# Values of two heads projected as a pair, token blocks stationary, in a one-core decoder layer

## The chip, the core and the metric

The kernel runs on one core of one Trainium2 chip. The metric is device time in microseconds, lower is better. Before the change it took 2126.11 us, the median of three runs that lie between 2125.86 and 2126.69 us.

## The reference, cut to what matters

One layer on 512 tokens of width 2048, all in float32: RMS norm, one wide input projection, 16 attention heads of 128 columns, output projection with residual, RMS norm, gated feed-forward network with residual.

```python
proj = h @ w_in          # h = rms_norm(x); columns are split by head
qf, kf, vf, ff, qn, kc, vc, ks, vs, kw, vw, gt = jnp.split(proj, cuts, axis=-1)
# 8 "fox" heads: q, k normalised per head, forgetting attention
qf = _rms_norm(qf.reshape(B, T, Hf, Dh), fox_q_norm)
kf = _rms_norm(kf.reshape(B, T, Hf, Dh), fox_k_norm)
vf = vf.reshape(B, T, Hf, Dh)                       # values: no norm
# 8 "nsa" heads in 2 groups: compressed (kc, vc), selected (ks, vs) and
# window (kw, vw) branches, summed with sigmoid gates gt
o_nsa = g[..., 0:1] * o_c + g[..., 1:2] * o_s + g[..., 2:3] * o_w
x = x + concat(o_fox, o_nsa) @ w_out
x = x + (silu(h2 @ w_gate) * (h2 @ w_up)) @ w_down  # h2 = rms_norm(x)
```

There are twelve value projections: `vs` and `vw` for each of the two groups, and `vf` for each of the eight fox heads.

## The kernel before, in words

Every matrix is split into a high part (rounded to the matmul's reduced float32 form) and a low part (the rest), and a product is three matmuls: high by high, high by low, low by high (`mm3`, L146 to L150). The split takes one ScalarE copy and one VectorE subtraction (`split`, L128; the lines of the profile are L80 and L77, in the helpers `act` and `tt`).

The input is held transposed, in 16 chunks `xg[k]` of 128 columns by 512 tokens, inside one large tile `bigm`. A projection of one head (`proj` and `gemm_steps`) streams its weights in two loads of 128x1024 (`load_w`: three landing buffers `ws`, two split buffers `wp`). Each 128x128 weight block is the stationary operand and the 512 tokens move: 16 chunks by 3 products are 48 matmuls of 512 columns. The result stands in PSUM as head columns by tokens, in one of two banks `g`. `scaled` (L270) multiplies it on VectorE by the tokens' row factor `rstd`. Queries and keys then pass `normed`: square, sum over columns by a matmul with ones (`ss`, L232 and L233), `rsqrt` (three ScalarE steps L222 to L224, three VectorE steps L225 to L227), gain (L295), split. Values need tokens on the partitions, so `value` transposes the scaled tile with four TensorE transposes (`vT`, L310) into a PSUM bank `t` and splits that.

The attention part runs in a written order of generators. `weave` interleaves the steps of a projection with those of an attention head, `stagger` starts the next projection before the rest of the last one (`POST`) is done, `run` takes all steps at once. A scheduling layer places the instructions of each engine, and on each engine they execute in that order. The order before: `ks0`; `vs0`, `kw0`, `vw0` beside the compression of `kc` and `vc` (`windows`, `compress`, whose matmuls `z` are L410); `qn0` beside the gates; the nsa heads 0 to 3, each beside the next projection; `vs1`, `kw1`, `vw1`, `qn4` one after the other; nsa heads 4 to 7; then for each fox head its query, key and value projection beside the attention of the head before. At the end the 16 head outputs are split into `bigm` (these splits wait for the last head's scaled scores, `scores_done`), and the output projection `po` starts, its first two accumulators in the banks `g`.

The feed-forward part behind it (`q`, L976, and `pd`, L1111 and L1116) is not edited. Its matmuls have 256 moving columns, one stationary block each.

Of the kernel before, what the change touches and what calls it, by code (L numbers as in the profile page):

```python
# [17 lines left out]
P = 128  # L18
# [38 lines left out]

SHIFT = 8


# [8 lines left out]
def hybrid_layer(ctx: ExitStack, tc: tile.TileContext, xT, vec, ffb, wfg, wfirst, win, cmpw, wout, wgu, wdn, out):  # L69
# [68 lines left out]

    def load_w(src, name):
# [40 lines left out]
    def gemm_steps(o, srcs, mov, name):  # L180

        k = 0
        for j, src in enumerate(srcs):
            wp = load_w(src, f"{name}_{j}")
            for kk in range(src.shape[-1] // P):
                s = slice(kk * P, (kk + 1) * P)
                mm3(o, wp[:, 0, s], wp[:, 1, s], mov[k][:, 0, :], mov[k][:, 1, :],
                    k == 0, k == len(mov) - 1)
                k += 1
                yield  # L190
        assert k == len(mov)

    def gemm2(os, srcs, mov, name):

        for j in range(4):
            st = wpl.tile([P, HALF * P], F32, tag="ws", name=f"ws_{name}_{j}", bufs=3)
            for i in range(2):
                load(st[:, i * T:(i + 1) * T], srcs[i][j // 2][:, j % 2 * T:(j % 2 + 1) * T])
            wp = wpl.tile([P, 2, HALF * P], FR, tag="wp", name=f"wp_{name}_{j}", bufs=2)
            split(wp, st)  # L200
            for kk in range(4):
                k = 4 * j + kk
                for i in range(2):
                    c = slice(i * T + kk * P, i * T + (kk + 1) * P)
                    mm3(os[i], wp[:, 0, c], wp[:, 1, c], mov[k][:, 0, :], mov[k][:, 1, :], k == 0, k == len(mov) - 1)

# [12 lines left out]

    def rsqrt(dst, src, n, tmp):  # L220
# [5 lines left out]
        nc.vector.tensor_scalar(tmp, tmp, -0.5 / n, 1.5, op0=OP.mult, op1=OP.add)  # L226
        nc.vector.tensor_tensor(dst, dst, tmp, op=OP.mult)  # L227

# [32 lines left out]
    gneg = ap_.tile([P, 2], F32, name="gneg")  # L261
    nc.vector.tensor_scalar_mul(gneg[:, 0:1], v1(V_FQ), -SCALE)
    nc.vector.tensor_scalar_mul(gneg[:, 1:2], v1(V_NQ), -SCALE)

# [18 lines left out]
    def normed(name, gain, tag, bufs):  # L283
# [9 lines left out]
        y = ftile(f"y_{name}")  # L293
        rsqrt(y, o, float(HD), ftile(f"tmp_{name}"))
        nc.vector.scalar_tensor_tensor(t, t, gain, y, op0=OP.mult, op1=OP.mult)  # L295
# [7 lines left out]

    def value(name):

        t = yield from proj(name)
        yield POST
        o = ps.tile([P, T], F32, tag="t", name=f"vT_{name}", bufs=2)
        for i in range(NB):
            nc.tensor.transpose(o[:, i * P:(i + 1) * P], t[:, i * P:(i + 1) * P], ident)  # L310
        r = ap_.tile([P, 2, T], FR, tag="kv", name=name, bufs=5)
        split(r, o)
        live[name] = r

    class Branch:
# [41 lines left out]
        def pv(self, o, start, stop):  # L357
            v, pt = self.v, self.pt
            for n, j in enumerate((0, 1, 3, 2)):
                c = slice(TOFF[j], TOFF[j] + T - j * P)  # L360
                vs = slice(j * P, (j + 1) * P)
                mm3(o[:, j * P:], v[:, 0, vs], v[:, 1, vs], pt[:, 0, c], pt[:, 1, c],
                    start and n == 0, stop and n == NB - 1)
                yield
# [198 lines left out]
    def nsa_q(h):  # L563
        return normed(f"qn{h}", gneg[:, 1:2], "q", 2)

# [8 lines left out]
    for k in range(NK):  # L574
# [5 lines left out]
        split(t, xs, v1(V_AN + k))  # L580
        wp = wpl.tile([P, 2, HALF * P], FR, tag="wp", name=f"w0p_{k}", bufs=2)
        w_done = split(wp[:, :, :T], ws)
        if k == 0:
            wst = wpl.tile([P, HALF * P], F32, tag="ws", name="ws_fg", bufs=3)[:, :NK * 32]
            nc.sync.dma_start(wst, wfg)
            wst = wst.rearrange("p (k c) -> p k c", c=32)
            wf = wpl.tile([P, NK, 2, 32], FR, tag="wp", name="wf", bufs=2)
            nc.scalar.activation(wf[:, :, 0], wst, AF.Copy)
# [15 lines left out]

    ks0 = normed("ks0", v1(V_SK), "kv", 5)
    next(ks0)
    row_rstd("r1")

    def unload():
        for j, which in enumerate(("kc", "vc")):  # L610
# [6 lines left out]
        tokens["fg"] = fg  # L617
        yield

    N, NS, F, FS = 18, 26, 53, 12  # L620
    weave(ks0, unload(), N, 5, 9)
# [3 lines left out]
    weave(nsa_q(0), gates(), N, 4, 2)  # L625
    for h in range(3):
        weave(nsa_q(h + 1), nsa(h), N, NS, 7, 17)
    weave(normed("ks1", v1(V_SK), "kv", 5), nsa(3), N, NS, 7, 17)
# [6 lines left out]
    def qk(h):  # L635
        return stagger(normed(f"qf{h}", gneg[:, 0:1], "q", 2), normed(f"kf{h}", v1(V_FK), "kv", 5))

    weave(qk(0), nsa(7), 2 * N - 1, NS, 6)
    run(stagger(value("vf0")))
    run(late[0])  # L640
    for h in range(NH - 3):
        weave(chain(qk(h + 1), stagger(value(f"vf{h + 1}"))), fox(h), F - 2, FS, 4, 0)

    h = NH - 1
    weave(qk(h - 1), fox(h - 2), 2 * N - 1, FS, 4, 0)
    side = fox(h - 1)
    weave(qk(h), itertools.islice(side, 5), 2 * N - 1, 5, 12)
    weave(stagger(value(f"vf{h - 1}")), itertools.islice(side, 2), N - 1, 2, 8)
    last = fox(h)
    for i, _ in enumerate(stagger(value(f"vf{h}"))):  # L650
        if i in (2, 4, 6, 8, 10):
            next(last)
        if i in (7, 9, 11, 13, 15):
            next(side, None)
    run(late[0])
    run(side)
# [20 lines left out]
    formy = ffp.tile([P, 2 * FORM], FR, tag="fy", name="formy", bufs=1)  # L677

    def cut(m, at, n):
        return m[:, at:at + n]  # L680

# [208 lines left out]
    def load_a(i):  # L890
# [5 lines left out]
        if i == 2:  # L896
            tc.add_manual_dep(d.ins, live["w0"].ins.name, PACE)

    def split2(dst, src):
        h = act(dst[0], src, AF.Copy)  # L900
        tt(dst[1], src, dst[0].bitcast(F32), op=OP.subtract)
        return h

# [308 lines left out]
```

## Time and profile before

| | |
|---|---|
| time of the profiled execution | 2126.17 us |
| its span, first to last instruction | 2124.5 us |
| so outside the span | 1.67 us |
| median of three runs | 2126.11 us |
| TensorE (PE) busy | 2110.1 us, 15135 matmuls |
| VectorE (DVE) busy | 1696.7 us |
| ScalarE (ACT) busy | 996.3 us |
| granted TensorE clock, mean | 0.999 |

Stages by time from the span's start: input and `kc`, `vc`, gate projections to 58 us, the attention part to about 690 us, the output projection to 875 us, gate and up products to 1697 us, down product to the end. In lists of single instructions the first column is the start and the second the duration, both in us. Matmuls are pipelined, so a duration overlaps the next instruction; what a matmul costs is the distance from its start to the next start.

### The profile page before, as it was taken

To read this page: it belongs to the slowest core of one execution; us is meant where nothing else is said; L and a number is where in the kernel's file an instruction comes from. 1 tells how busy PE (TensorE), PEld (TensorE's weight loads), DVE (VectorE), ACT (ScalarE), POOL (GpSimd) and SP (SyncE) were. 2 spreads that over 40 slices of the span, in tenths; PEclk is the share of its full clock that TensorE was granted. 3 is DMA by queue.
4 is the path that set the end of the run, shared out by engine and by line. 5 is a ranking of instruction groups with operands and counts; after the bars stand their busy time and mean duration, and the time that the engine had idled before them with its cause. 6 is when DMAs were issued, how large, how long until landed. Compare 5 with 4: busy or idle time off the path is not lost.

```text
span 2124.5 us, 36976 instructions
## 1 busy us (share of the span) xinstructions
PE 2110.1 (99%) x15135; PEld 1949.7 (92%) x15135; DVE 1696.7 (80%) x2488; ACT 996.3 (47%) x1226; POOL 184.2 (9%) x283
## 2 busy tenths in 40 slices
PE   9999999999999999999999999999999999999998
PEld 7777787888888888999999999999999999999998
DVE  6877568555657454999999999999999987889998
ACT  5555455444446333544344434343443455565553
POOL 0000000111101000111111111111111000000000
PEclk9999999999999999999999999999999999999999
DMA  5421211222222443667676777777777798469864
GB/s 195 149 75 50 61 60 45 85 85 89 86 85 67 157 143 124 169 190 210 185 199 188 186 199 188 200 189 183 204 189 197 230 334 266 150 234 331 291 180 138
DMA packets 113483, 349.57 MB, mean 165 GB/s; under 512 B 13592, under 2 KB 13592, under 8 KB 113312
## 3 DMA queue, kind: packets, MB, share of 16 engines
q1 hardware_dynamic: 85552, 270.33, 38.6%
q0 software_dynamic: 22144, 52.44, 13.5%
q10 hardware_dynamic: 5616, 24.43, 2.9%
q8 instruction: 118, 1.93, 0.4%
q14 instruction: 53, 0.43, 0.1%
HBM read 318.56 MB, written 74.73 MB: 185 GB/s over the span
## 4 chain that ended last, share of the span: by engine, by line
PE 93%; DVE 4%; ACT 2%; issue 1%; DMA 1%; ACTq 0%; SPq 0%; DVEq 0%
PE q L976 39%; PE pd L1111 13%; PE pd L1116 6%; PE po L150 2%; PE po L148 2%; PE po L149 2%; PE ps_kf L148 1%; PE ps_kf L150 1%; PE ps_kf L149 1%; PE ps_qf L148 1%; PE ps_vf L148 1%; PE ps_qf L150 1%; PE ps_qf L149 1%; PE ps_vf L150 1%; PE ps_vf L149 1%; PE ps_qn L150 1%
## 5 line engine op out<-in xcount | busy, mean ns | idle before, releaser
L80 ACT ACTIVATE bigm<-r 128x1792 fp32r<-128x1792 f32 x174 | 298.2, 1714 | 460.4 <-PE q L976 289.9
L77 DVE TENSOR_TENSOR bigm<-r,bigm 128x1792 fp32r<-128x1792 f32 x174 | 351.5, 2020 | 12.1 <-ACT bigm L80 11.5
L77 DVE TENSOR_TENSOR r<-r 128x512 f32<-128x512 f32 x522 | 267.1, 512 | 28.7 <-DMA r<-wgu 16.6
L976 PE MATMUL q<-bigm 128*128 128x256 f32 x1848 | 217.4, 276 | 0.1
L976 PE MATMUL q<-formy,bigm 128*128 128x256 f32 x1848 | 216.8, 276 | 0.0
L976 PE MATMUL q<-forma,bigm 128*128 128x256 f32 x1848 | 216.8, 276 | 0.0
L976 PE MATMUL q<-formx,bigm 128*128 128x256 f32 x1848 | 216.8, 276 | 0.0
L976 PEld LDWEIGHTS q<-bigm 128*128 128x128 f32 x1848 | 213.2, 188 | 0.4 <-DVE bigm L77 0.3
L976 PEld LDWEIGHTS q<-forma,bigm 128*128 128x128 f32 x1848 | 213.0, 188 | 0.1
L976 PEld LDWEIGHTS q<-formy,bigm 128*128 128x128 f32 x1848 | 212.9, 188 | 0.1
L976 PEld LDWEIGHTS q<-formx,bigm 128*128 128x128 f32 x1848 | 212.9, 188 | 0.0
L122 POOL DMA_DIRECT2D wsum<-wdn x176 | 119.8, 687 | 880.5 <-ACT bigm L80 775.9
L1111 PE MATMUL pd<-bigm 128*128 128x256 f32 x1224 | 147.9, 276 | 0.0
L1111 PEld LDWEIGHTS pd<-bigm 128*128 128x128 f32 x1224 | 142.9, 188 | 0.0
L77 DVE TENSOR_TENSOR bigm<-wd,bigm 128x2048 fp32r<-128x2048 f32 (+1 forms) x64 | 110.2, 1723 | 12.9 <-ACT bigm L80 12.7
L80 ACT ACTIVATE bigm<-rawm 128x768 fp32r<-128x768 f32 (+2 forms) x72 | 65.9, 925 | 108.0 <-PE pd L1116 62.7
L148 PE MATMUL po<-bigm,wp_o 128*128 128x512 f32 x256 | 99.9, 390 | 0.7 <-ACT wp_o L80 0.6
L150 PE MATMUL po<-bigm,wp_o 128*128 128x512 f32 x256 | 99.6, 390 | 0.2 <-DVE wp_o L77 0.2
L149 PE MATMUL po<-bigm,wp_o 128*128 128x512 f32 x256 | 99.6, 389 | 0.0
L77 DVE TENSOR_TENSOR bigm<-rawm,bigm 128x768 fp32r<-128x768 f32 (+2 forms) x72 | 75.3, 1055 | 26.4 <-ACT bigm L80 25.6
L80 ACT ACTIVATE bigm<-wd 128x2048 fp32r<-128x2048 f32 (+1 forms) x64 | 93.2, 1456 | 6.0 <-DVE wd L77 2.5
L1116 PE MATMUL pd<-bigm 128*128 128x256 f32 x612 | 81.1, 276 | 0.0
(487 smaller groups left out, 4060.1 us busy)
## 6 DMA issues: line engine op xcount, KB each, us to landing
r<-wgu SPq DMA_DIRECT2D x174, 512.0 KB, 4.2
wsum<-wdn POOLq DMA_DIRECT2D x176, 256.0 KB, 4.9
rawm<-ad SPq DMA_DIRECT2D x44, 512.0 KB, 6.6
wd<-wdn SPq DMA_DIRECT2D x40, 512.0 KB, 5.9
wd<-wsum SPq DMA_DIRECT2D x40, 512.0 KB, 7.0
ad<-cb ACTq DMA_DIRECT2D x22, 896.0 KB, 5.5
rawm<-ad SPq DMA_DIRECT2D x44, 384.0 KB, 3.3
ws_o<-wout SPq DMA_DIRECT2D x28, 512.0 KB, 3.6
```

The costliest lines, as they stand in the source:

```text
L77: return pin(nc.vector.tensor_tensor(*args, op=op))
L80: return pin(nc.scalar.activation(*args, **kw))
L122: d = nc.gpsimd.dma_start(step[0], step[1], **step[2])
L148: nc.tensor.matmul(o, lh, rh, start=start, stop=False)
L149: nc.tensor.matmul(o, lh, rl, start=False, stop=False)
L150: nc.tensor.matmul(o, ll, rh, start=False, stop=stop)
L976: nc.tensor.matmul(o, w[wp][:, fb, cs], a[:, xp, fa], start=(k == 0 and h == 0 and wp == 0 and xp == 0), stop=(g == NG - 1 and kk == 1 and ...
L1111: nc.tensor.matmul(b[q][k][:, h * 256:(h + 1) * 256], w[0][:, fb, q * P:(q + 1) * P], a[xp][:, fa], start=(j == 0 and h == 0 and xp == 0), ...
L1116: nc.tensor.matmul(b[q][k][:, h * 256:(h + 1) * 256], w[1][:, fb, q * P:(q + 1) * P], a[0][:, fa], start=False, stop=(j == NJ - 1), skip_g ...
```

## The change

The two heads of a value pair, `vs`/`vw` of a group or two neighbouring fox heads, are projected together by `values`. A block of 128 tokens of `xg[k]` is now the stationary operand and 256 weight columns, 128 of each head, move. A pair takes 4 token blocks by 16 chunks by 3 products, 192 matmuls of 256 columns, into both `g` banks (token blocks 0 and 1 in the first, 2 and 3 in the second). The result has tokens on the partitions, so the transposes and `scaled` are dropped; the row factor is applied in the split, per partition, from a small tile `rcol` that four small transposes of `rstd` fill once. The two parts of a weight tile get fixed offsets (`VOFF`, `SHIFT`) for the pairs. `rsqrt` in `normed` drops one VectorE step, its factor going into the gains. The order changes: the pair goes ahead of `kw`, the gates come between the two compressions, the second group's projections are staggered, fox projections are regrouped around the pairs, and the last pair runs beside the heads 6 and 7. Five of the output splits wait for head 6's scores (`early`) instead of head 7's, and the first two `po` accumulators lie in the banks `s`. The host orders the weight columns accordingly.

```diff
+VOFF = 48
...
+    def split2(dst, src, scale=None):
+        if scale is None:
+            h = act(dst[0], src, AF.Copy)
+            tt(dst[1], src, dst[0].bitcast(F32), op=OP.subtract)
+        else:
+            h = act(dst[0], src, AF.Copy, scale=scale)
+            nc.vector.scalar_tensor_tensor(dst[1], src, scale, dst[0].bitcast(F32), op0=OP.mult, op1=OP.subtract)
+        return h
...
-        wp = wpl.tile([P, 2, HALF * P], FR, tag="wp", name=f"wp_{name}", bufs=2)
-        split(wp[:, :, :n], st[:, :n])
+        wp = parts_tile(f"wp_{name}")
+        hi, lo = 0, n
+        if off:
+            hi, lo = n + VOFF, VOFF - (SHIFT if off > 1 else 0)
+        wp = [cut(wp, at, n) for at in (hi, lo)]
+        split2(wp, st[:, :n])
...
-        nc.vector.tensor_scalar(tmp, tmp, -0.5 / n, 1.5, op0=OP.mult, op1=OP.add)
-        nc.vector.tensor_tensor(dst, dst, tmp, op=OP.mult)
+        if whole:
+            nc.vector.tensor_scalar(tmp, tmp, -0.5 / n, 1.5, op0=OP.mult, op1=OP.add)
+            nc.vector.tensor_tensor(dst, dst, tmp, op=OP.mult)
+        else:
+            nc.vector.scalar_tensor_tensor(dst, tmp, -3.0 * n, dst, op0=OP.add, op1=OP.mult)
...
-    def value(name):
-        t = yield from proj(name)
-        yield POST
-        o = ps.tile([P, T], F32, tag="t", name=f"vT_{name}", bufs=2)
-        for i in range(NB):
-            nc.tensor.transpose(o[:, i * P:(i + 1) * P], t[:, i * P:(i + 1) * P], ident)
-        r = ap_.tile([P, 2, T], FR, tag="kv", name=name, bufs=5)
-        split(r, o)
-        live[name] = r
+    def values(pair):
+        z = [ps.tile([P, T], F32, tag="g", name=f"ps_{pair[0]}{b}", bufs=2) for b in range(2)]
...
+        for c in range(4):
+            wp = load_w(win[i + c // 2, c % 2], f"{pair[0]}_{c}", 1 if c else 2)
+            for b in range(2):
+                for kk in range(4):
+                    x = xg[4 * c + kk]
+                    ws = slice(kk * 2 * HD, (kk + 1) * 2 * HD)
+                    for t in range(2):
+                        at = slice((2 * b + t) * P, (2 * b + t + 1) * P)
+                        for n, (xp, w) in enumerate(((0, 0), (0, 1), (1, 0))):
+                            nc.tensor.matmul(z[b][:, t * 2 * HD:(t + 1) * 2 * HD], x[:, xp, at], wp[w][:, ws], ...
+                    yield
+                if c == 3:
+                    r = ap_.tile([P, 2, T], FR, tag="kv", name=f"{pair[0]}{b}", bufs=5)
+                    for t in range(2):
+                        ts = slice(t * 2 * HD, (t + 1) * 2 * HD)
+                        split2([r[:, p, ts] for p in range(2)], z[b][:, ts], rcol[:, 2 * b + t:2 * b + t + 1])
...
+        tr = ps.tile([P, NB, NH], F32, tag="t", name="ps_rT", bufs=2)
+        for i in range(NB):
+            nc.tensor.transpose(tr[:, i, :], rstd[:NH, i * P:(i + 1) * P], ident[:NH, :NH])
+        nc.vector.tensor_copy(rcol, tr[:, :, 0])
...
-    weave(stagger(value("vs0"), normed("kw0", v1(V_WK), "kv", 5), value("vw0")),
-          chain(windows("kc", V_PK), compress("kc"), windows("vc", V_PV), compress("vc")), 3 * NK, 74, 3)
+    weave(stagger(values(("vs0", "vw0")), normed("kw0", gain(V_WK), "kv", 5), nsa_q(0)),
+          chain(windows("kc", V_PK), compress("kc"), gates(), windows("vc", V_PV), compress("vc")), 4 * NK, 78, 3)
...
-    run(value("vs1"))
-    run(normed("kw1", v1(V_WK), "kv", 5))
-    run(value("vw1"))
-    run(nsa_q(4))
+    run(stagger(values(("vs1", "vw1")), normed("kw1", gain(V_WK), "kv", 5), nsa_q(4)))
...
+    for h in range(0, 6, 2):
+        weave(stagger(qf(h + 1), kf(h + 1), qf(h + 2)), fox(h), F - 2, FS, 4, 0)
+        if h < 4:
+            weave(stagger(kf(h + 2), vf(h + 2)), fox(h + 1), F - 4, FS, 4, 0)
+        else:
+            weave(stagger(kf(h + 2), qf(h + 3), kf(h + 3)), fox(h + 1), F - 2, FS, 4, 0)
...
-        tc.add_manual_dep(split(t, oT[h]).ins, scores_done.ins.name, PACE)
+        tc.add_manual_dep(split(t, oT[h]).ins, (early if i < 5 else scores_done).ins.name, PACE)
...
-    both_z = [ps.tile([P, T], F32, tag="g", name=f"po{n}", bufs=2) for n in (0, HALF)]
+    both_z = [ps.tile([P, T], F32, tag="s", name=f"po{n}", bufs=2) for n in (0, HALF)]
```

More of the change, by code (lines that the diff above doesn't have):

```diff
@@ L198, in gemm2 @@
                 load(st[:, i * T:(i + 1) * T], srcs[i][j // 2][:, j % 2 * T:(j % 2 + 1) * T])
-            wp = wpl.tile([P, 2, HALF * P], FR, tag="wp", name=f"wp_{name}_{j}", bufs=2)
-            split(wp, st)
+            wp = parts_tile(f"wp_{name}_{j}")
+            wp = [cut(wp, at, HALF * P) for at in (0, HALF * P)]
+            split2(wp, st)
             for kk in range(4):
@@ L602, in hybrid_layer @@
         xg.append(t)
-    ks0 = normed("ks0", v1(V_SK), "kv", 5)
+    ks0 = normed("ks0", gain(V_SK), "kv", 5)
     next(ks0)
@@ L633, in hybrid_layer @@
+    run(stagger(values(("vs1", "vw1")), normed("kw1", gain(V_WK), "kv", 5), nsa_q(4)))
+    run(late[0])
     for h in range(4, 7):
         weave(nsa_q(h + 1), nsa(h), N, NS, 7, 17)
[L635 to L651, printed above, removed]
+    def qf(h):
+        return normed(f"qf{h}", gain(V_FQ), "q", 2)
+    def kf(h):
+        return normed(f"kf{h}", gain(V_FK), "kv", 5)
+    def vf(h):
+        return values((f"vf{h}", f"vf{h + 1}"))
@@ new lines, in hybrid_layer @@
+    weave(stagger(qf(0), kf(0)), nsa(7), 2 * N - 1, NS, 6)
+    run(stagger(vf(0)))
+    for h in range(0, 6, 2):
[4 more added lines that the diff above has]
+            weave(stagger(kf(h + 2), qf(h + 3), kf(h + 3)), fox(h + 1), F - 2, FS, 4, 0)
+    side, last = fox(NH - 2), fox(NH - 1)
+    for i, _ in enumerate(stagger(vf(NH - 2))):
+        if 2 <= i < 18 and i % 2 == 0:
+            next(side)
+            if i == 12:
+                early = live["scaled"]
+        if 18 <= i < 28 and i % 2 == 0:
@@ L652, in hybrid_layer @@
             next(last)
-        if i in (7, 9, 11, 13, 15):
-            next(side, None)
-    run(late[0])
     run(side)
@@ L1195 @@
         "wfirst": wi[:, cut["kc"]:cut["kc"] + 4 * P].reshape(NK, P, 4 * P),
-        "win": _tiles(np.concatenate(cols, axis=1), np),
+        "win": win,
         "cmpw": np.concatenate(cw, axis=0),
```

70 lines of the change are left out of this document (43 added, 27 removed).

## The prediction

> **What bounds the kernel now.** I read the page first: busy time, the clock row, the chain that ended last.
>
> ```profile
> PE 2110.1 (99%) x15135; PEld 1949.7 (92%) x15135; DVE 1696.7 (80%) x2488; ACT 996.3 (47%) x1226; POOL 184.2 (9%) x283
> ...
> PEclk9999999999999999999999999999999999999999
> ...
> PE 93%; DVE 4%; ACT 2%; issue 1%; DMA 1%; ACTq 0%; SPq 0%; DVEq 0%
> ```
>
> TensorE is busy for 99% of the span at the full granted clock, and the chain is TensorE for 93%. A change can win here only by taking work from TensorE or by closing one of its few gaps. It loses where it makes TensorE wait. Next come the busy times by stage (stretch, length, then busy us and counts of PE, PEld, DVE, ACT, POOL).
>
> ```profile
> 69.00:107.00 38.00, 36.17 (x182) 29.42 (x181) 34.05 (x52) 24.27 (x45) 0.00 (x0) 1.00 0.38 126
> ...
> 136.00:236.00 100.00, 98.81 (x529) 79.19 (x527) 80.17 (x227) 58.51 (x132) 2.47 (x4) 1.00 0.14 43
> ...
> 300.00:660.00 360.00, 359.75 (x1748) 295.67 (x1747) 223.27 (x459) 175.53 (x326) 39.80 (x61) 1.00 0.24 77
> 875.00:1697.00 822.00, 821.87 (x7246) 821.61 (x7245) 778.13 (x1040) 338.81 (x249) 118.09 (x173) 1.00 0.73 193
> ```
>
> The reader is to see three kinds of stretch. From 300 to 660 us, where most fox heads lie, TensorE has no idle time (359.75 of 360) and VectorE has 38% to spare. From 136 to 236 us, the first nsa heads, TensorE idles 1.2 of 100 us. From 69 to 107 us, where the first value projections stand beside the compression, VectorE is busy 34.05 of 38 us, 90%: there TensorE can be held up by VectorE's queue. The feed-forward part from 875 us on is not edited and I give it no change.
>
> **Rates of the matmuls.** The new form is 256 moving columns with a new stationary block each time. The chain has a long unbroken run of that shape, and the timeline of TensorE has the old form and another 256-column form (`z_kc`).
>
> ```profile
> 887.46 809.86 PE q L976 x7140
> ...
> 507.50 0.39 PE L148 MATMUL ps_vf<-bigm,wp_vf 128*128 128x512 f32 x1
> ...
> 509.55 0.40 PE L232 MATMUL ss_kf<-fr_kf,ones 128*128 128x512 f32 x1
> ...
> 514.27 0.44 PE L148 MATMUL ps_vf<-bigm,wp_vf 128*128 128x512 f32 x1
> ...
> 517.10 0.28 PE L148 MATMUL of<-pt_f,vf 128*128 128x256 f32 x1
> ...
> 88.94 1.10 PE L410 MATMUL z_kc<-wp_kc,xb_kc 128*128 128x256 f32 x8
> 89.88 0.40 PE L149 MATMUL ps_kw<-bigm,wp_kw 128*128 128x512 f32 x1
> ```
>
> The run gives 809.86 / 7140 = 113.4 ns per 256-column matmul. In the old value projection nine matmuls take 509.55 - 507.50 = 2.05 us (228 ns each) and twelve take 517.10 - 514.27 = 2.83 us (236 ns); I take 231 ns. The eight `z_kc` matmuls take 0.94 us, 117.5 ns each. So a shape has two prices, 113.4 and 117.5, and the trace does not say which one the pairs get. I choose 113.4 because the pairs read their moving operand from one contiguous run, as `q` does, while a `z_kc` matmul gathers 128 columns from each of two parts; 117.5 stays as the upper bound.
>
> **The change part by part.** Streaming: a pair before is 96 matmuls of 231 ns, 22.18 us; after, 192 of 113.4 ns, 21.77 us. That is -0.41 us, and over six pairs -2.5 us. The first quarter's low parts are shifted by eight elements; at the `z_kc` price its 16 matmuls per pair add 16 x 4.1 ns, 0.4 us over six pairs. Term: **-2.1 us**. If all 1152 run at 117.5, they cost 1152 x 4.1 ns = 4.7 us more than at 113.4. On the low side, 236 ns for the old form gives -5.3 us.
>
> The pairs load a stationary block 1152 times where 576 did before. The row that bears on it is the load itself:
>
> ```profile
> L976 PEld LDWEIGHTS q<-bigm 128*128 128x128 f32 x1848 | 213.2, 188 | 0.4 <-DVE bigm L77 0.3
> ```
>
> A load lasts 188 ns, yet the loads of `q` fit in a spacing of 113.4 ns, so they overlap the running matmuls, and I price the extra 576 at nothing: the running matmul is their cover, and uncovered they would cost 576 x 188 ns = 108 us. [...]
>
> Transposes: removed are 48 `vT` matmuls, added are four with eight moving columns for `rcol`, whose nearest row is `ps_cq`, the same shape.
>
> ```profile
> 90.34 0.60 PE L310 MATMUL vT_vs<-ident,t_vs 128*128 128x128 f32 x4
> 90.70 0.48 PE L148 MATMUL ps_kw<-bigm,wp_kw 128*128 128x512 f32 x1
> ...
> L512 PE MATMUL ps_cq<-ident,cum x4: 201/202/223, 128.1 to 128.3; 8*128 8x8 f32 x4
> ```
>
> Four transposes take 0.36 us from start to start; twelve values make **-4.3 us**, on TensorE itself and so on the path. The four of `ps_cq` start within 0.2 us; with the step behind them I put **+0.3 us**.
>
> A new wait at the first pair: in the changed order of VectorE the low part of the pair's third weight load stands behind four `wp_kc` splits; before, the second projection's first load (`wp_kw`) stood ahead of them. These are TensorE's and VectorE's rows there.
>
> ```profile
> 69.32 0.39 PE L148 MATMUL ps_vs<-bigm,wp_vs 128*128 128x512 f32 x1
> ...
> 83.14 0.39 PE L149 MATMUL ps_kw<-bigm,wp_kw 128*128 128x512 f32 x1
> 84.50 0.71 PE L410 MATMUL z_kc<-wp_kc,qq 128*128 128x256 f32 x4 [0.97 <-ACT wp_kc L80]
> ...
> 76.25 0.42 DVE L226 TENSOR_SCALAR tmp_ks<-tmp_ks 128x512 f32<-128x512 f32 x1
> 76.58 1.13 DVE L385 TENSOR_TENSOR xt_kc<-t_kc,vt 128x512 f32<-128x512 f32 x1
> ...
> 78.13 1.23 DVE L77 TENSOR_TENSOR wp_kw<-ws_kw,wp_kw 128x1024 fp32r<-128x1024 f32 x1
> 79.27 0.76 DVE L295 SCALAR_TENSOR_TENSOR t_ks<-t_ks,vt,y_ks 128x512 f32<-128x512 f32 x1
> ...
> 84.85 2.51 DVE L77 TENSOR_TENSOR wp_kc<-ws_kc,wp_kc 128x512 fp32r<-128x512 f32 x4
> ```
>
> The fourth `wp_kc` split is the third of the last row (each about 0.6 us), done near 86.7. After the change `wp_kw` (79.27 - 78.13 = 1.14 us) and the dropped step (76.58 - 76.25 = 0.33 us) no longer precede it and a small copy does (0.1): 85.3. The third load's low part then takes 1.23 us: 86.6. TensorE starts the pair at 69.32 + 0.3, runs half of it (96 x 113.4 ns = 10.9 us) and two `ss` matmuls (0.45): 81.0. All it can do until 86.6 is 16 `z_kc` and two pair matmuls, 16 x 117.5 + 2 x 113.4 ns = 2.1 us. It waits 3.5 us, where the rows before show 84.50 - 83.14 less one matmul, 1.1 us: +2.4. Behind it the gates stand between the two compressions, so `zkT` and `z_vc` wait for a longer VectorE queue; those waits are not in the trace of before. I bound them by zero and by another 2.4, and take 0.6. Term: **+3.0 us**, from 0 (if TensorE makes it up by waiting less later) to +5.
>
> Bank eviction: both `g` banks are held until a pair ends. The next projection needs the first one 24 matmuls later, 2.72 us.
>
> ```profile
> L80 ACT ACTIVATE pt_f<-pT_f 128x256 fp32r<-128x256 f32 x8 | 2.9, 368 | 0.0
> ...
> L77 DVE TENSOR_TENSOR ca<-q,ca 128x256 f32<-128x256 f32 x30 | 12.5, 418 | 0.1
> ...
> L80 ACT ACTIVATE wp_vf<-ws_vf 128x1024 fp32r<-128x1024 f32 x16 | 16.8, 1053 | 16.1 <-PE ps_kf L150 16.1
> L77 DVE TENSOR_TENSOR wp_vf<-ws_vf,wp_vf 128x1024 fp32r<-128x1024 f32 x16 | 19.6, 1224 | 24.9 <-ACT wp_vf L80 24.9
> ```
>
> In the new order the second ScalarE copy of a bank waits for VectorE's first subtraction, so four steps follow each other: 2 x (0.368 + 0.418) = 1.57 us. That is inside 2.72, and the weight split ahead of it in both queues is started a quarter of a pair earlier. I price it at nothing; without that cover it costs what the queue exceeds 1.15 us.
>
> Norms: each of 28 loses a VectorE step and changes another.
>
> ```profile
> L226 DVE TENSOR_SCALAR tmp_kf<-tmp_kf 128x512 f32<-128x512 f32 x8 | 3.4, 424 | 0.2
> ...
> L227 DVE TENSOR_TENSOR y_kf<-y_kf,tmp_kf 128x512 f32<-128x512 f32 x8 | 5.5, 692 | 0.2
> ...
> L270 DVE TENSOR_TENSOR t_vf<-ps_vf,rstd 128x512 f32<-128x512 f32 x8 | 5.5, 685 | 0.1
> ```
>
> 28 x 0.424 us and twelve `scaled` of 0.685 us leave VectorE, 20 us, almost all of it where TensorE never waits. The exception is the nsa heads: 1.2 us of idle per 100 us there, some 2.4 over eight heads. I take **-1.0 us**, from 0 to -2.4.
>
> Tail: the list of waits of TensorE shows what the last heads leave.
>
> ```profile
> PE po L148 <- ACT wp_o L80: 0.6, 1, 0.6
> ...
> PE vT_vf L310 <- DVE t_vf L270: 0.3, 1, 0.3
> ...
> PE po L148 <- DVE x L77: 0.2, 1, 0.2
> PE po L150 <- DVE wp_o L77: 0.2, 1, 0.2
> ```
>
> The `vT` wait goes, and five early splits let `wp_o` come sooner: of 1.3 us I take **-1.1**. What is late next is head 7's `pt` split behind the output splits on ScalarE; a whole wait for it would turn the term to +1.
>
> Sum: -2.1 - 4.3 + 0.3 + 3.0 - 1.0 - 1.1 = **-5.2 us**. The profiled execution took 2126.17 us (span 2124.5 and 1.67 outside), 0.06 above the median, so I forecast 2121.0 us.
>
> **Rivals.** *The other price* (0.15): the pairs run at 117.5 ns. The two-part gather speaks against it, the equal roles of the operands (tokens stationary, weights moving) for it. The sum is -0.5: 2125.7 us.
>
> *Waits eat the gain* (0.18): in the stretch that VectorE fills to 90%, what TensorE saves comes back as waits, and the first pair's term reaches +5, with the tail at +1: -5.2 + 2.0 + 2.1, about 2125 us. The busy share speaks for it, the idle VectorE from 300 us on against.
>
> *Eviction late* (0.08), the slower side: at a pair's end two weight splits and one step of a norm stand ahead of the eviction on VectorE, 2 x 1.224 + 0.692 + 1.57 = 4.7 us against 2.72, so TensorE waits 2.0 us per pair and 12 us over six: -5.2 + 12 = +6.8, 2133 us. Slower than before begins above 5.2 / 6 = 0.9 us lost per pair, at 3.6 us from last matmul to free bank; slower by more than can be told from no change at 1.6 us lost. The new order shows one split ahead, and that one started early, which speaks against it; the shared bank makes the four steps serial, which speaks for it.
>
> *Loads not hidden* (0.01): 2121.0 + 108 = 2229 us.
>
> **How the numbers follow.** This kernel's measurement can tell about 0.2%, 4.25 us: faster ends at 2121.9. My forecast case (0.58) lies on the faster side, but only by a microsecond, and its own terms spread it from 2115.5 (old form at 236 ns, no wait at the first pair) to 2124. The two cases without much gain hold 0.33 and lie within 0.2%. Late eviction and exposed loads, 0.09, are put on the slower side. The range 2115.5 to 2126.0 takes in the forecast's spread and the two middle cases.
>
> **What would show it.** Right: no `vT` rows, pair matmuls starting 113 to 114 ns apart, one wait of about 3.5 us before the third quarter of the first pair, released by VectorE's split of `wp_vs`, and TensorE without idle from 300 to 660 us. Wrong: a spacing near 118 ns, gaps behind each pair's last matmul released by the split of `vf`, or idle of TensorE in the nsa heads well above 2.4 us.

## The result and the profile after

| | before | after |
|---|---|---|
| median, us | 2126.43 | 2123.45 |
| range of the runs, us | 2125.68 to 2138.11 | 2122.12 to 2124.80 |
| ratio, 95% interval | | 0.9983 (0.9976 to 0.9990) |
| profiled execution, us | 2126.17 | 2123.22 |
| its span, us | 2124.5 | 2121.5 |

One more run of the kernel before, 2159.92 us, was in a slower state and counts for neither the range nor the ratio. The change makes the kernel 3.0 us faster by the medians, 0.14%; the ratio is one of means and counts the run of 2138.11 us, hence its 0.17%. The forecast of 2121.0 us had the direction; its size, 5.2 us, was too large. The time lies inside the range, but within the 0.2% to which the prediction gave 0.33; the case that it held more likely (0.58), faster by more than that, did not come. The interval still sets the time apart from no change. The page of the kernel after, busy times and chain:

```profile
PE 2105.8 (99%) x15667; PEld 1974.1 (93%) x15667; DVE 1683.4 (79%) x2462; ACT 999.5 (47%) x1238; POOL 189.1 (9%) x283
...
PE 83%; issue 10%; DVE 3%; ACT 1%; POOL 1%; DMA 0%; ACTq 0%; POOLq 0%; SPq 0%; DVEq 0%
```

TensorE is still busy for 99% of the span, and VectorE has lost 13 us. The chain's "issue 10%" is the way in which it was followed: from a late transpose of a fox head it runs back to GpSimd, while TensorE works on. The stretches of the kernel after (stretch, length, then busy us and counts of PE, PEld, DVE, ACT, POOL; the last is shifted by 3 us so that it holds the same work):

```profile
69.00:107.00 38.00, 35.62 (x266) 32.80 (x265) 25.50 (x41) 20.70 (x40) 0.00 (x0) 1.00 0.45 150
136.00:236.00 100.00, 99.38 (x555) 81.69 (x555) 79.65 (x226) 61.43 (x137) 2.49 (x4) 1.00 0.13 43
300.00:660.00 360.00, 358.08 (x2057) 308.71 (x2056) 215.10 (x434) 178.45 (x333) 43.41 (x61) 1.00 0.24 78
872.00:1694.00 822.00, 821.97 (x7247) 821.70 (x7246) 778.50 (x1040) 338.41 (x249) 118.40 (x173) 1.00 0.73 193
```

The nsa heads (136 to 236) idle less, 0.6 us in 100. The fox heads, which hardly idled (0.25 us), now idle 1.9 us of 360. The feed-forward part is unchanged.

Where the time arises is read at four matmuls that have the same work ahead of them in both kernels: the first of `qn3`, the first of `qn5`, the norm sum of `qf0`, and the first of the output projection's third accumulator. TensorE's rows of the kernel before (start, duration):

```profile
171.19 0.47 PE L148 MATMUL ps_qn<-bigm,wp_qn 128*128 128x512 f32 x1
...
275.88 0.39 PE L148 MATMUL ps_qn<-bigm,wp_qn 128*128 128x512 f32 x1
...
388.00 0.39 PE L232 MATMUL ss_qf<-fr_qf,ones 128*128 128x512 f32 x1
...
704.85 0.47 PE L148 MATMUL po<-bigm,wp_o 128*128 128x512 f32 x1 [0.20 <-DVE x L77]
```

The same four in the kernel after:

```profile
172.44 0.48 PE L170 MATMUL ps_qn<-bigm,wp_qn 128*128 128x512 f32 x1
...
275.63 0.39 PE L170 MATMUL ps_qn<-bigm,wp_qn 128*128 128x512 f32 x1
...
387.74 0.40 PE L258 MATMUL ss_qf<-fr_qf,ones 128*128 128x512 f32 x1
...
701.86 0.39 PE L170 MATMUL po<-bigm,wp_o 128*128 128x512 f32 x1
```

The kernel after is 1.25 us behind at the first point, 0.25 us ahead at the second and third, 2.99 us ahead at the fourth. So the first stretch loses 1.25 us, the nsa heads with the second pair gain 1.5, the fox heads with four pairs and the tail gain 2.7. Within a stretch, the distance from each matmul's start to the next start, summed by what it computes, gives the terms:

| term | forecast | measured | where |
|---|---|---|---|
| streaming of the value projections | -2.1 | +1.8 | +0.5, +0.6, +0.7 in the three stretches |
| 48 transposes removed | -4.3 | -4.8 | -0.9, -0.8, -3.05 |
| transposes of `rcol` | +0.3 | +0.3 | first stretch |
| rest of the first stretch (new waits) | +3.0 | +1.1 | to 172 us |
| rest of the nsa heads (norms) | -1.0 | -1.3 | to 388 us |
| rest of the fox heads and the tail | -1.1 | -0.4 | to 702 us |
| start of the run | 0 | +0.15 | the loop ahead of `ks0` |
| sum, read at the fourth matmul (the rows are rounded) | -5.2 | -3.0 | |

One term has the wrong sign, the streaming: it came out 3.9 us worse than forecast. It is in all three stretches, and it is the first thing that the experiments ask about. The total missed by only 2.2 us because other terms, the new waits of the first stretch above all, came out better; that is luck, not foresight.

### The profile page after: what moved, and what is told of

Same layout as the page of the kernel before. It is cut to its first block, busy times and chain, and to the rows that moved or that the text cites. A ratio compares the mean times of both kernels' runs of the same rounds, so it can differ in the third digit from the quotient of the medians.

```text
span 2121.5 us, 38029 instructions
## 1 busy us (share of the span) xinstructions
PE 2105.8 (99%) x15667; PEld 1974.1 (93%) x15667; DVE 1683.4 (79%) x2462; ACT 999.5 (47%) x1238; POOL 189.1 (9%) x283
## 4 chain that ended last, share of the span: by engine, by line
PE 83%; issue 10%; DVE 3%; ACT 1%; POOL 1%; DMA 0%; ACTq 0%; POOLq 0%; SPq 0%; DVEq 0%
PE q L1027 39%; PE pd L1162 13%; PE pd L1167 6%; PE po L171 3%; PE po L172 3%; PE po L170 3%; PE ps_vs L351 2%; PE ps_vf L351 1%; PE ps_qn L171 1%; PE ps_qn L172 1%; PE ps_qn L170 1%; POOL nbf L596 1%; PE ps_first L170 1%; PE ps_first L172 1%; PE ps_first L171 1%
## 5 line engine op out<-in xcount | busy, mean ns | idle before, releaser
L1162 PE MATMUL pd<-bigm 128*128 128x256 f32 x1224 | 147.9, 276 | 0.0
L351 PE MATMUL ps_vf<-wp_vf,bigm 128*128 128x256 f32 x768 | 95.5, 280 | 0.0
```

What stands on the lines that cost most here:

```text
L351: nc.tensor.matmul(z[b][:, t * 2 * HD:(t + 1) * 2 * HD], x[:, xp, at], wp[w][:, ws], start=(c == 0 and kk == 0 and t == 0 and n == 0), sto ...
L1162: nc.tensor.matmul(b[q][k][:, h * 256:(h + 1) * 256], w[0][:, fb, q * P:(q + 1) * P], a[xp][:, fa], start=(j == 0 and h == 0 and xp == 0), ...
```

## Experiments: two spacings

Each time is a median; the ratio is one of means, to the kernel before, run beside it on the same chip. The kernel before had medians of 2126.38 to 2126.72 us there, so edited kernels that ran on different chips can be compared to some 0.3 us.

In the kernel after the pair matmuls have two spacings. Two pairs run with nothing between their matmuls, at the same addresses: `vs1` and `vf0`. Their last stretch and the projection behind it, from the timeline of the kernel after:

```profile
241.81 11.71 PE L351 MATMUL ps_vs<-wp_vs,bigm 128*128 128x256 f32 x98
253.35 0.39 PE L170 MATMUL ps_kw<-bigm,wp_kw 128*128 128x512 f32 x1
...
399.76 10.70 PE L351 MATMUL ps_vf<-wp_vf,bigm 128*128 128x256 f32 x93
410.30 0.39 PE L170 MATMUL ps_qf<-bigm,wp_qf 128*128 128x512 f32 x1
```

(253.35 - 241.81) / 98 = 117.8 ns, (410.30 - 399.76) / 93 = 113.3 ns. Of the 1152 pair matmuls 444 start 113.4 ns apart on average, 642 117.7 ns; 59 take about 150 ns, nearly all of them at or within three matmuls of a switch to or from another tile, and seven hold a wait. Without the waits the mean is 117.7 ns, where the forecast had 113.4 with 0.35 for the shifted quarter.

**The offsets left out** (`flat`).

```diff
-wp = load_w(win[i + c // 2, c % 2], f"{pair[0]}_{c}", 1 if c else 2)
+wp = load_w(win[i + c // 2, c % 2], f"{pair[0]}_{c}", 0)
```

> The changed kernel with the two parts of the pairs' weight tiles at plain offsets (high part at 0, low part at 1024), so without VOFF and SHIFT. In the changed kernel the pair matmuls start 113.3 ns apart in some stretches and 117.8 ns apart in others, 117.7 ns on average with the switches between tiles. Theory 1, the place decides: at plain offsets no stretch runs at 113.3 ns; some 420 of the 1152 pair matmuls lose 4.5 ns or more, so the time is about 1.9 us above the changed kernel, 2125.3 us. Theory 2, only what ran just before decides: the same mixture of the two spacings, and the time of the changed kernel, 2123.4 us.

Measured: 2126.57 us, ratio 1.0 (0.9992 to 1.0009), 3.1 us above the kernel after. `vs1` in its trace:

```profile
241.78 12.76 PE L351 MATMUL ps_vs<-wp_vs,bigm 128*128 128x256 f32 x105
254.38 0.40 PE L170 MATMUL ps_kw<-bigm,wp_kw 128*128 128x512 f32 x1
```

That is 120.0 ns. Of the 1152 only 16 are near 113, 1040 are at 119.5 ns. Theory 1 holds, and the loss is larger than it said (1.9 us) because the matmuls at 117.8 ns lost too: the place of the operands decided here whether TensorE kept the short spacing (16 matmuls near it in place of 444). Without the offsets the whole gain of the change is gone, though the 48 transposes stay away.

**The shift left out** (`noshift`).

```diff
-wp = load_w(win[i + c // 2, c % 2], f"{pair[0]}_{c}", 1 if c else 2)
+wp = load_w(win[i + c // 2, c % 2], f"{pair[0]}_{c}", 1)
```

> The changed kernel without SHIFT: the low part of each pair's first quarter lies 48 elements into its tile as in the other three quarters. Theory A, each matmul has its own price by its operands' places: the first quarters, 117.6 ns a matmul now, go to the price of the others, 113.3 to 117.8, which takes 0 to 1.2 us off; the other quarters stay as they are. Theory B, the shifted quarter is a kick that throws TensorE from the slow spacing into the fast one, which it then keeps: without it no quarter gets to 113.3 ns, the second, third and fourth quarters go to 117.8, and the time rises by about 1.9 us to 2125.3 us.

Measured: 2123.38 us, 0.9985 (0.9976 to 0.9994), as the kernel after. In the trace 585 matmuls are at 113.4 ns in place of 444: the first quarters go from 117.7 to 116.9 ns on average, and `vs1` now runs at 113.3 from its second quarter on, (252.89 - 239.75) / 116:

```profile
239.75 13.31 PE L351 MATMUL ps_vs<-wp_vs,bigm 128*128 128x256 f32 x116
252.89 0.39 PE L170 MATMUL ps_kw<-bigm,wp_kw 128*128 128x512 f32 x1
```

Theory B falls, the shift is no kick that is needed. That `vs1` changed with it is not in theory A either, nor that the second quarter of `vs0` went the other way, from 113.4 to 117.8 ns. The 0.7 us that the spacings gain in the trace don't show in the medians.

**Two split buffers an even multiple of 512 bytes apart** (`stride`).

```diff
-        return wpl.tile([P, 2 * HALF * P + P], FR, tag="wp", name=name, bufs=2)
+        nparts[0] += 1
+        return wpl.tile([P, 2 * HALF * P + P], FR, tag=f"wp{nparts[0] % 2}", name=name, bufs=1)
...
-    ident = pers.tile([P, P], F32, name="ident")
+    first_parts = parts_tile("w0p_0")
+    ident = wpl.tile([P, P], F32, tag="id", name="ident", bufs=1)
```

> The changed kernel with its two weight split buffers an even multiple of 512 bytes apart (the identity tile lies between them) instead of an odd one; nothing else differs. In the changed kernel the woven pairs vf2, vf4 and vf6 run at 117.8 ns in the first and third quarter (one buffer) and at 114.2 to 116 in the second and fourth (the other). Theory C, the place modulo 1024 bytes decides into which spacing TensorE falls after it has been at another tile: both buffers now have the place of the first one, so all four quarters of these pairs run near 117.8, about 0.5 us worse for each of the three. Theory D, the buffers' place has no part in it: the quarters stay as they are and the time too.

Measured: 2137.82 us, 1.0054 (1.0042 to 1.0067), 14.4 us above the kernel after. But 11.4 us of the loss arise in the first loop, ahead of `ks0`, which the planner ordered otherwise (below), and some 3 us behind the start of the output projection, where `q` has listed waits of 2.6 us. The pairs answer the question: `vf2` has 117.9, 114.4, 117.8, 114.8 ns in its four quarters, against 117.8, 114.4, 117.9, 114.8 in the kernel after. Theory C falls, the buffer's place modulo 1024 has no part in it. `vs1` ran at 113.3 and `vf0` at 117.8, both exchanged against the kernel after.

**The kernel after once more** (`again`).

> The changed kernel once more, unedited. In its first trace the two pairs that run with nothing between their matmuls keep one spacing to the end: vs1 117.8 ns from its second quarter on, vf0 113.3 ns in its last half. In four kernels that differ elsewhere, one or the other had the other spacing at the same addresses. Theory 1, the program sets it: both pairs show the same spacings again. Theory 2, it is settled anew in each execution: at least one of the two changes, and the times spread by the price of such a switch, 0.6 us a pair, within 2122.1 to 2124.8 us.

Measured: 2123.52 us, 0.9986 (0.9975 to 0.9996). `vs1` in its trace:

```profile
242.76 12.41 PE L351 MATMUL ps_vs<-wp_vs,bigm 128*128 128x256 f32 x104
255.01 0.39 PE L170 MATMUL ps_kw<-bigm,wp_kw 128*128 128x512 f32 x1
```

117.8 ns again, and `vf0` 113.3 again. Theory 1 holds for these two pairs: over two executions the program set the spacing, and an edit elsewhere can exchange it. It doesn't hold for all: in the woven pairs the second quarters of `vf2` and `vf4`, at 114.4 and 115.9 ns in the first trace, are at 115.9 and 114.4 in this one. The span of this execution was 2.8 us longer than that of the first one. 1.7 us of that lie ahead of `qn3`, and 1.2 of these in long distances between the first loop's matmuls; so part of the spread of the runs arises there, not in the pairs.

**Attention steps two at a time, the shorter last** (`short`, without the shift).

```diff
-            for i in reversed(range(NB)):            # scores of f1, f3, f6, f7
+            for i in (3, 0, 2, 1):                   # a yield after 0 and after 1
-            for n, j in enumerate((0, 1, 3, 2)):     # products
+            for n, j in enumerate((0, 3, 1, 2)):     # a yield after 3 and after 2
```

> The kernel without SHIFT, and with the attention steps that stand between the matmuls of the pairs vf2, vf4 and vf6 taken two at a time with the shorter one last (512 then 128 columns, 384 then 256); the transposes of these heads come later. In the traces so far these pairs run at 117.8 ns after a step of 512 or 384 columns and at 113.3 after one of 128 or 256, in every kernel with the pairs' offsets. Theory 1, the step before decides: now every stretch of these pairs but those behind a projection or the norm's sums runs at 113.3 ns, which takes 0.4 to 0.5 us off each of the three, three switches fewer take 0.2 us more, and the waits for the transposes of f1, f3 and f6 (0.37, 0.37, 1.2 us) go: about 3.5 us below the kernel without SHIFT, 2119.9 us. Theory 2, the quarter (its buffer) decides: first and third quarters stay at 117.8 ns, and only switches and waits go: 2.3 us below, 2121.1 us.

Measured: 2122.11 us, 0.9985 (0.9972 to 0.9999; the ratio counts one run of 2139.66 us), 1.3 us below `noshift`. Neither theory holds. Behind 512 and 128 columns of the product `vf2` runs at 113.4 ns (third quarter, 117.9 before), behind 384 and 256 at 117.8, and the last pair lost its short spacing behind head 7's scores. The count at 113.4 ns fell from 585 to 453 (`vs1` went back to 117.8). What was gained came from the waits: those for the transposes of f1 and f3 are gone, the one of f6 fell from 1.17 to 0.64 us. What sets the spacing after a step of another tile stays open; the size of the last step alone doesn't.

## Experiments: the other terms

**The transposes alone** (`notrans`), in the kernel before.

```diff
-        for i in range(NB):
-            nc.tensor.transpose(o[:, i * P:(i + 1) * P], t[:, i * P:(i + 1) * P], ident)
-        split(r, o)
+        split(r, t)
```

> The kernel before with the 48 value transposes left out: the scaled tile is split as it stands, so the values enter the product untransposed. In the trace of before these 48 rows take 4.76 us from start to start, and the matmuls ahead of them start 0.66 us later than they could. Theory 1, they lie on TensorE's path: 5 us less, about 2121.2 us. Theory 2, something else of the same step is late anyway (VectorE's scaled tile, the split of the value): less than 2 us of it shows, 2124.5 us or more.

Measured: 2121.74 us, 0.9978 (0.9969 to 0.9987), 4.85 us less. Theory 1 holds, the transposes are on the path at their full price. This is more than the whole change brings.

**Half of the windows of `kc` taken earlier** (`start`).

```diff
-    weave(ks0, unload(), N, 6, 9)
+    wkc = windows("kc", V_PK)
+    weave(ks0, chain(unload(), itertools.islice(wkc, 2)), N, 8, 9)
...
-          chain(windows("kc", V_PK), compress("kc"), ..., 4 * NK, 78, 3)
+          chain(wkc, compress("kc"), ..., 4 * NK, 76, 3)
```

> The changed kernel with half of the windows of kc (the VectorE and ScalarE steps xt_kc and qq) taken into the stretch of ks0, where VectorE idles 2.1 us and then 1.6 us; nothing else differs. In the changed kernel TensorE waits 2.7 us at the first pair's third quarter for wp_kc, xb_kc and wp_vs. Theory 1: VectorE's queue between 75 and 88 us sets this wait, and about 1.5 us of it goes: 2121.9 us. Theory 2: the stretch to 136 us is bound by VectorE's work as a whole, and the wait appears again at zkT, z_vc or the first scores: 2123.4 us.

TensorE in the kernel after, at the first pair:

```profile
80.80 1.07 PE L351 MATMUL ps_vs<-wp_vs,bigm 128*128 128x256 f32 x8
83.24 0.71 PE L460 MATMUL z_kc<-wp_kc,qq 128*128 128x256 f32 x4 [1.37 <-ACT xb_kc L438]
83.79 0.28 PE L351 MATMUL ps_vs<-wp_vs,bigm 128*128 128x256 f32 x1
83.91 0.63 PE L460 MATMUL z_kc<-wp_kc,qq 128*128 128x256 f32 x4
85.04 1.31 PE L460 MATMUL z_kc<-wp_kc,qq 128*128 128x256 f32 x8 [0.50 <-DVE wp_kc L79]
86.69 1.53 PE L351 MATMUL ps_vs<-wp_vs,bigm 128*128 128x256 f32 x11 [0.33 <-DVE wp_vs L79]
```

And VectorE's row that the forecast worked out, with the one that stood in its way:

```profile
83.60 0.69 DVE L439 TENSOR_TENSOR xb_kc<-xt_kc,xb_kc 128x512 fp32r<-128x512 f32 x1
...
85.41 1.22 DVE L79 TENSOR_TENSOR wp_vs<-ws_vs,wp_vs 128x1024 fp32r<-128x1024 f32 x1
```

With the edit, VectorE does two windows at 69.77 and the first `z_kc` in the trace of `start` waits 0.73 us, the only listed wait there:

```profile
82.76 0.74 PE L460 MATMUL z_kc<-wp_kc,qq 128*128 128x256 f32 x4 [0.73 <-DVE wp_kc L79]
```

Measured: 2120.59 us, 0.9972 (0.9961 to 0.9983), 2.9 us below the kernel after; all its runs (2119.49 to 2121.38) lie below the fastest of that kernel. Theory 1 holds, and the gain is larger than it said: the first stretch is 3.5 us shorter in the trace (0.6 of it the start of the run). `vs1` fell into the short spacing and `vf0` into the long one, 0.6 us each, which cancel. The stretch was not bound by the amount of VectorE's work but by when it was done.

**The norm's step back** in the kernel after (`norms`), and **the norm part alone** in the kernel before (`normsonly`: the change's `rsqrt` and `gains`, nothing else).

```diff
-        rsqrt(y, o, float(HD), ftile(f"tmp_{name}"), False)
+        rsqrt(y, o, float(HD), ftile(f"tmp_{name}"))
...
-    nc.vector.tensor_scalar_mul(gains, vt[:, 0:6], -0.5 / HD)
+    nc.vector.tensor_scalar_mul(gains, vt[:, 0:6], 1.0)
```

> The changed kernel with the norm's dropped VectorE step put back (28 norms) and the gains unscaled. Theory 1: the step sits in front of the nsa heads' waits, so what it saved there comes back, about 1.0 us by the sum of the prediction (0 to 2.4): 2124.4 us, seen as longer waits of TensorE between 136 and 390 us. Theory 2: the shorter waits of the nsa heads come from the pairs and the new order, and VectorE has room for the step: less than 0.3 us, 2123.5 us.

> The kernel before with the norm part of the change alone: one VectorE step less in each of 28 norms, its factor in the gains; everything else as before. Theory 1, the term of the prediction: shorter waits of TensorE in the nsa heads, 1.0 us less, 2125.4 us. Theory 2, a step of 0.42 us off VectorE is worth 0.3 us at most there (undone in the changed kernel it cost no more by the trace): 2126.1 us or above.

Measured: `norms` 2121.51 us, 0.9977 (0.9968 to 0.9987), 1.9 us *below* the kernel after; `normsonly` 2127.29 us, 1.0005 (0.9995 to 1.0014), 0.75 us above the kernel before, which its interval can't tell from none. Seven of the nine runs of `norms` lie below the fastest of the kernel after. Neither theory has a gain for `norms`. `normsonly` lies where its theory 2 has it, but not for that reason. From `qn3` to the norm sum of `qf0`, the nsa heads, `normsonly` is 1.5 us shorter than the kernel before, as the prediction's term has it. But it loses 2.6 us before, and its waits say where:

```profile
PE z_kc L417 <- ACT xb_kc L395: 1.5, 1, 1.5
PE z_kc L417 <- DVE wp_kc L77: 0.6, 1, 0.6
```

These are the two `z_kc` waits of the kernel after, in a kernel that has no pair. In the kernel before eleven matmuls of `kw0` ran ahead of the first `z_kc`, in `normsonly` only two: with the dropped step the planner put `z_kc` so early on TensorE that its operands were not ready. The granted clock was lower there too, 0.96 on average from 69 to 107 us (1.00 in the kernel before), so not all of the 2.6 us need be waits. In `norms` twelve more pair matmuls than in the kernel after stand ahead of the first `z_kc`, and one listed wait of 1.6 us is left.

**The last pair's side steps later** (`tail`).

```diff
-        if 2 <= i < 18 and i % 2 == 0:
+        if i in (2, 4, 6, 8, 10, 14, 16, 18):
             next(side)
-            if i == 12:
+            if i == 14:
                 early = live["scaled"]
-        if 18 <= i < 28 and i % 2 == 0:
+        if i in (12, 20, 22, 24, 26):
             next(last)
```

> The changed kernel with the last pair's side steps placed otherwise: head 6's transposes two steps later, head 7 two steps later. In the changed kernel's trace TensorE waits 1.17 us for head 6's scaled scores (before its first transpose) and 0.58 us for the split of the last values. Theory 1: the first of the two goes, 1.1 us less, 2122.3 us. Theory 2: what is late is the queue of ScalarE and VectorE as a whole, and the same time comes back at the next product or at the first output projection: 2123.4 us.

Measured: 2123.93 us, 0.9987 (0.9979 to 0.9996): no gain. TensorE in `tail`, around head 6's first transpose:

```profile
655.83 3.96 PE L351 MATMUL ps_vf<-wp_vf,bigm 128*128 128x256 f32 x33
660.80 0.63 PE L403 MATMUL pT_f<-ident,p_f 128*128 128x128 f32 x4 [1.01 <-DVE p_f L391]
```

And in the kernel after:

```profile
655.38 3.96 PE L351 MATMUL ps_vf<-wp_vf,bigm 128*128 128x256 f32 x33
660.35 0.84 PE L403 MATMUL pT_f<-ident,p_f 128*128 128x128 f32 x6 [1.01 <-DVE p_f L391]
```

The planner had already put the transpose behind 33 pair matmuls, and the written step moved nothing. The edit didn't do what it says, so it decides between neither theory.

**The gains together** (`best`): the edit of `start`, no shift, the steps of f1 and f3 as in `short`, and the last pair's side steps one at a time, as follows.

```diff
-        if 2 <= i < 18 and i % 2 == 0:
+        if i in (2, 4, 6, 8, 10, 17, 20, 23):
             next(side)
-            if i == 12:
+            if i == 17:
                 early = live["scaled"]
-        if 18 <= i < 28 and i % 2 == 0:
+        if i in (12, 18, 21, 24, 26):
             next(last)
```

> The changed kernel with four edits together: half of kc's windows in the stretch of ks0, no SHIFT, the steps of heads f1 and f3 two at a time beside their pairs, and beside the last pair head 6's transposes five steps later with head 7's first scores ahead of them. Theory 1, the gains add: 2120.6 us (the first edit alone) less 1.3 (the second and third) less about 0.6 (half of the wait for head 6's scores), 2118.7 us. Theory 2, the later edits only move the waits, and what SHIFT and the steps gave was the chance spacing of two pairs: 2120.6 us, as with the first edit alone.

Measured: 2118.79 us, 0.9965 (0.9952 to 0.9977), 7.7 us below the kernel before and 4.7 below the kernel after. Its slowest run, 2119.41, lies below the fastest of the kernel after, 2122.12. The time is where theory 1 has it. Part of that is the chance of which theory 2 speaks: against `start` the fox heads and the tail are 2.6 us shorter in the trace, and 0.6 of this is `vf0`, which is back at the short spacing. TensorE's longest waits in the kernel after:

```profile
PE ps_warm L619 <- DVE pc L285: 1.8, 1, 1.8
PE pT_f L403 <- DVE p_f L391: 1.4, 3, 1.0
PE z_kc L460 <- ACT xb_kc L438: 1.4, 1, 1.4
PE z_kc L460 <- DVE wp_kc L79: 0.5, 1, 0.5
```

And in `best`:

```profile
PE ps_warm L622 <- DVE pc L285: 1.8, 1, 1.8
PE z_kc L463 <- DVE wp_kc L79: 0.8, 1, 0.8
PE q L1031 <- ACT bigm L82: 0.6, 2, 0.3
PE of L170 <- ACT vf L82: 0.4, 1, 0.4
```

The waits for `p_f` are no longer among the listed ones, and `z_kc` waits 0.8 us in place of 1.9. `vs1` runs at the short spacing, (249.69 - 235.75) / 123 = 113.3 ns:

```profile
235.75 14.10 PE L351 MATMUL ps_vs<-wp_vs,bigm 128*128 128x256 f32 x123
249.69 0.39 PE L170 MATMUL ps_kw<-bigm,wp_kw 128*128 128x512 f32 x1
```

Of the 1152 pair matmuls 714 are at 113.4 ns.

**`best` with the norm's step back** (`bestnorms`), by the two edits of `norms`.

> The four edits of the run before (kc's windows earlier, no SHIFT, steps of f1 and f3 two at a time, the last pair's side steps later), with the norm's dropped VectorE step put back. Alone in the kernel before, the dropped step cost 0.7 us: the nsa heads waited less, but the planner's order of the first stretch got worse. Theory 1: with that stretch mended by the first edit only the gain in the nsa heads is left, so putting the step back costs 0.5 to 1.9 us, 2119.3 to 2120.7 us. Theory 2: the step is worth nothing by itself, and each order is its own draw: within 0.3 us of 2118.8 us, or below.

Measured: 2119.85 us, 0.9967 (0.9955 to 0.9980), 1.06 us above `best`, which the intervals alone don't separate. In the trace the first stretch and the nsa heads are 1.3 us longer, 0.4 of it the start of the run. Another 1.1 us comes from the fox heads, where `vf0` went to the long spacing and the last pair's wait rose, 0.6 us each. The size fits theory 1, and with the first stretch mended the dropped step is worth about 0.9 us where the prediction placed it; but the fox heads' part is not in that theory, so the run doesn't settle it.

## Why the prediction was right or wrong

**The bound** was right. Work taken from TensorE showed in full (`notrans`, 4.85 us), the feed-forward part didn't change, and a reordered first stretch was paid for in waits.

**Streaming** is the step that failed: "I choose 113.4 because the pairs read their moving operand from one contiguous run, as `q` does". A contiguous run isn't enough. `flat` reads the same contiguous runs and never settles at 113.4 (1040 of its 1152 are at 119.5 ns). With the offsets the short spacing is possible, but the pairs have it for 444 of 1152 matmuls. `q` averages it over 7140 in a row; that nothing comes between can't be the whole reason, since `vs1` ran 98 in a row at 117.8. The old form also cost more than the 231 ns assumed, 232.3 over the 570 without a wait. New form 1152 x 117.7 ns = 135.6 us, old form 133.8: +1.8 in place of -2.1. The rival *the other price* had the right mean, but as one price for the shape, where there are two spacings and the switches; its reason, the equal roles of the operands, no run asked about. Its sum, 2125.7, was wrong since the terms beside it came out lower.

**Weight loads**: hidden, as forecast. In the last half of `vf0` in the kernel after, from 399.5 to 410.3 us, each load of a 128x128 block lasts 187 to 188 ns and the matmuls start 113.3 ns apart. The 108 us of the rival *loads not hidden* did not come.

**Transposes**: 4.8 us where 4.3 was put, the right mechanism a little under-sized: the 0.36 us came from one of the shorter groups. `rcol`: as forecast.

**The first pair's wait**: VectorE's third `wp_vs` split was forecast to be done at 86.6 us, and 85.41 + 1.22 is 86.63. TensorE came to that point 0.9 us later than worked out, because it started at 69.90 and ran at 117 ns, and so waited 2.7 us from start to start, not 3.5. The larger part stood elsewhere than forecast, ahead of `z_kc`, released by `xb_kc`. The further 0.6 us for the compressions did not come: the kernel before has listed waits of 0.3 us for `zkT` and 0.6 for `z_vc`, the kernel after 0.4 for `z_vc` alone. The whole stretch lost 1.1 us in place of 3.0. `normsonly` shows that the `xb_kc` wait needs no pair: the dropped norm step is enough for it.

**Bank eviction**: nothing behind a pair's last matmul while another projection follows, as forecast. Only the last pair's values, which head 6 needs at once, are waited for (0.58 us from start to start). In the first bank of `vs1` the four steps do follow each other: they start at 250.73, 251.24, 251.75 and 252.26 us. They were put too low, though: in `vs` they take 0.475 and 0.482 us each, and behind `vs1` a weight split stands between them. The rival *eviction late* had none of its 2.0 us per pair.

**Norms**: -1.3 in the nsa heads against -1.0, and `normsonly` has -1.5 there. What the step failed to say is that dropping an instruction also changes the planner's order elsewhere, and that this can cost more than the step is worth.

**Tail**: -0.4 for the fox heads and the tail, against -1.1. The listed waits of `po` and `vT` did go. In their place came two of 0.37 us for `p_f` of f1 and f3, 1.17 us for that of f6 and 0.3 us at `vf0`: VectorE is late with the scaled scores of f1, f3 and f6, not ScalarE with head 7's `pt`. So "TensorE without idle from 300 to 660 us" was wrong by 1.9 us.

## What to carry to other kernels

Before a projection is turned round to save transposes, measure how far apart its new matmuls start in the place and the company in which they will stand: the spacing of another stage with the same shape was the best case here, not the price (113.4 ns in `q`, 117.7 ns on average in the pairs). After any edit under a planner, compare TensorE's waits in stretches that the edit doesn't touch; here a dropped VectorE step was worth 1.5 us where it was meant and cost 2.6 us where it wasn't. Two windows of VectorE work moved into its idle time gave 2.9 us, as much as the whole change.

## What the runs showed of the hardware

The same 256-column matmul at the same addresses had two spacings, 113.3 and 117.8 ns, and kept one for a hundred matmuls and more (123 at 113.3 ns in `best`, 104 at 117.8 in `again`). At the plain offsets of `flat` 1040 of the 1152 stand at one, 119.5 ns (120.0 in `vs1`). Over the nine kernels with pairs and offsets, `vs1` and `vf0` each had now the one and now the other: `vs1` 117.8 ns in the kernel after and 113.3 in `stride`, `vf0` 113.3 and 117.8. A second execution of the same program had the same ones for these two (117.8 and 113.3), but not for the second quarters of the woven `vf2` and `vf4` (114.4 and 115.9 ns, then 115.9 and 114.4). What selects the spacing stays open.

In `stride` the first loop waited for its input in many short gaps. TensorE's wait row, two of these waits, and the stretch behind them:

```profile
PE ps_first L648 <- DVE bigm L138: 2.8, 7, 0.6
...
16.06 0.68 PE L648 MATMUL ps_first<-bigm,wf 128*64 128x512 f32 x2 [0.60 <-DVE bigm L138]
...
18.59 0.68 PE L648 MATMUL ps_first<-bigm,wf 128*64 128x512 f32 x2 [0.59 <-DVE bigm L138]
```

```profile
20.00:30.00 10.00, 8.24 (x15) 2.49 (x16) 8.84 (x15) 7.39 (x13) 0.00 (x0) 0.50 1.00 349
```

The granted clock was 0.50 there (1.00 in the kernel after), and 1.00 again from 34 to 36 us. From the first warm-up matmul at 1.75 us to the drop, no listed wait is over 0.60 us, but from 16 to 20 us TensorE was busy for only 2.2 of 4 us. So here the clock's fall came after gaps of about 0.6 us; whether these lowered it was not shown, for no run varied them alone.
